# First stage of a hybrid decoder layer: x by token tile, conditioning in single chunks, loads in a fixed order

## The chip, the core and the metric

One core of a Trainium2 chip runs the whole layer in one launch. The metric is the device time of one execution in microseconds. TensorE (PE) multiplies into PSUM, VectorE (DVE), ScalarE (ACT) and GpSimd (POOL) work elementwise, SyncE (SP) issues most of the DMA loads.

## The reference

One layer of a decoder on x of 512 tokens by 1024, with a conditioning vector c of 1024. What the change touches is its beginning:

```
mod = silu(c) @ w_ada + b_ada            # w_ada: 1024 x 6144
shift_a, scale_a, gate_a, shift_f, scale_f, gate_f = split(mod, 6)
h = rms_norm(x, attn_norm) * (1 + scale_a) + shift_a
(nq, nkc, nvc, nks, nvs, nkw, nvw, ngate, cq, ckv, kr, bgate) = split(h @ w_in, ...)
```

After it come two attention branches (a sparse one with compressed, selected and window parts, and a latent one with a rotary key), gates, the output projection, and a gated MLP with a short causal convolution. Everything is float32; a product is made of three fp32r products of high and low halves (hi*hi, hi*lo, lo*hi).

## The kernel before

The kernel is written as a data flow of tiles. A planner orders the instructions of each engine ahead of the run, by priorities and its own estimate of times, and sets the semaphores; on the chip each engine runs its list in that order. `keep_in_program_order(ins)` binds an instruction behind the one that the program text traced before it on the same engine. `high_priority` moves it forward among those that are free to run.

The first stage computes the parts of `h @ w_in` that need all eight slices of 128 channels (k = 0 to 7) in seven PSUM banks at once: the gates and the latent query (408 columns, by token tile, banks bA) and the compressed keys and values (three of 128 columns, transposed, banks bF). Its pieces, in the text's order:

- x (eight DMAs of 256 KB, L417) is squared and summed per token, half on ACT (L437) and half on DVE (L434), the reciprocal root is taken on POOL for two token tiles at once (L135), and x is scaled. `x_half(i)` scales and transposes 512 channels of all four token tiles (L453, 16 transposes on PE) and copies them out of PSUM to xnT (L455). x_half(0) stands ahead of slice 0, x_half(1) behind its preparation.
- `mod_acc(j)` (L461) makes shift and scale for two slices at once: eight DMAs of 256 KB (L467: a row block of w_ada, two parts of 256 columns, 1 KB runs), and on DVE eight steps `acc = ada * csil[k] + acc` of 512 columns (L120, L122). The sum over the partitions follows in `mod_cols(j)` (L473): two f32 products with a column of ones on PE into a T bank, then mS and mA on DVE (L477 to L480).
- `prep(k)` calls both, loads and splits the weights of slice k (`load_w`: DMA at L112, high half by ACT at L83, low half by DVE at L84), issues late constants by the table LATE (L494), scales xnT[k] to h on ACT (L507) and splits h into hTh (ACT) and hTl (DVE).
- The loop at L517 calls prep(k + 1) and then issues slice k's 21 matmuls (L87): twelve of 408 columns and nine of 512.

The weight loads have 5 raw buffers, the conditioning loads 12 slots of 256 KB ("ml"), the split weights of this stage 10 ("cq"), the T banks of PSUM are two and one of them holds bF[2]. Only the late loads are bound to the text's order on SP. Behind the loop follow the latent query's norm, the second stage (banks bB, L555 on), the compressed branch, the eight heads and the MLP.

Of the kernel before, what the change touches and what calls it, by code (L numbers as in the profile page):

```python
# [10 lines left out]
F32 = mybir.dt.float32  # L11
# [6 lines left out]
P = 128  # L18
# [15 lines left out]
LATE = (0, 1, 1, 1, 2, 2, 2, 3, 3, 4, 5, 6, 7, 8, 9, 9, 9)  # L34
X_ACT = ((0, 0, 1, 1), (1, 1, 1, 1))
# [3 lines left out]
def tile_hybrid_layer(  # L39
# [18 lines left out]
    W_PRIO = [-50]  # L58
# [39 lines left out]

    @priority(lambda: W_PRIO[0])
    def load_w(segs, k0, kk, raw=None, tag=None):  # L100
        n = sum(g[2] for g in segs)
        assert kk * n <= 512
        raw = raw_unit() if raw is None else raw
        if tag:
            wh, wl = slot(tag, "wh", F32R), slot(tag, "wl", F32R)
        else:
            wh = wp.tile([P, 512], F32R, name="wh", tag="wh", bufs=4)
            wl = wp.tile([P, 512], F32R, name="wl", tag="wl", bufs=4)
        rv, hv, lv = (a[:, :kk * n].rearrange("p (k n) -> p k n", k=kk) for a in (raw, wh, wl))
# [299 lines left out]
    with tc.tile_pool(name="p1", bufs=1) as p1:  # L409
# [15 lines left out]
        vec.tensor_scalar(csil, csil, 0.5, None, op0=ALU.mult)  # L425

        ssh = sm.tile([P, NT, 2], F32, name="ssh")
        ssx = sm.tile([P, NT], F32, name="ssx")
        rsx = sm.tile([P, NT], F32, name="rsx")
        for t in range(NT):  # L430
            for i in range(2):
                if i:
                    scr = pj.tile([P, 512], F32, name="scr", tag="t2")
                    vec.tensor_tensor_reduce(scr, xt[t][i], xt[t][i], 1.0, 0.0, ALU.mult, ALU.add, ssh[:, t, i:i + 1])  # L434
                else:
                    scr = pj.tile([P, 512], F32, name="scr", tag="qg")
                    act.activation(scr, xt[t][i], AF.Square, accum_out=ssh[:, t, i:i + 1])  # L437
            if t % 2:
                t2 = slice(t - 1, t + 1)
                vec.tensor_add(ssx[:, t2], ssh[:, t2, 0], ssh[:, t2, 1])  # L440
                rstd(rsx[:, t2], ssx[:, t2], D, [P, 2])
        xnT = []

        def x_half(i):
            for t in range(NT):
                if X_ACT[i][t]:
                    act.activation(xt[t][i], xt[t][i], AF.Copy, scale=rsx[:, t:t + 1])
                else:
                    vec.tensor_scalar(xt[t][i], xt[t][i], rsx[:, t:t + 1], None, op0=ALU.mult)
            for k in range(4 * i, 4 * i + 4):  # L450
                tr = bank("T")
                for t in range(NT):
                    pe.transpose(tr[:, t * P:(t + 1) * P], xt[t][i][:, (k % 4) * P:(k % 4 + 1) * P], ident)  # L453
                xk = slot("KV", f"xnT{k}") if k < 6 else slot("KS", f"xnT{k}")[:, 0:512]
                act.activation(xk, tr, AF.Copy)  # L455
                xnT.append(xk)

        x_half(0)

        ACC = {}  # L460

        def mod_acc(j):
            if j % 2 == 0:
                acc = slot("U", "acc")
                for k in range(KD):
                    a = slot("ml", "ada")
                    dma(a.rearrange("p (s n) -> p s n", s=2),  # L467
                        w_ada[k * P:(k + 1) * P, 0:2 * D].rearrange("p (s n) -> p s n", s=2)[:, :, j * P:(j + 2) * P])
                    gemv_step(acc, a, k, True)
                for i in range(2):  # L470
                    ACC[j + i] = [acc[:, s * 256 + i * P:s * 256 + (i + 1) * P] for s in range(2)]

        def mod_cols(j):  # L473
            b = bank("T")
            for s in range(2):
                mm(b[:, s:s + 1], ACC[j][s], ones[:, 0:1], True, True)
            vec.tensor_add(mS[:, j:j + 1], b[:, 0:1], colA[:, 16 + j:17 + j])  # L477
            bp = sm.tile([P, 1], F32, name="bp")
            vec.scalar_tensor_tensor(bp, b[:, 1:2], 1.0, colA[:, 24 + j:25 + j], op0=ALU.add, op1=ALU.add)
            vec.tensor_mul(mA[:, j:j + 1], bp, colA[:, 8 + j:9 + j])  # L480
# [11 lines left out]
        def late_load(i):  # L492
            for dst, src in late[LATE[i]:LATE[i + 1]]:
                tc.keep_in_program_order(dma(dst, src))  # L494

        bA = [bank("G"), bank("G"), bank("S"), bank("S")]
        bF = [bank("O"), bank("F"), None]
        wk = {}

        def prep(k):  # L500
            mod_acc(k)
            mod_cols(k)
            wk[k] = (load_w([(w_in, O_NG, 408)], k, 1, slot("cq", "wr1")),
                     load_w([(w_in, O_KC, 384)], k, 1, slot("cq", "wr2")))
# [26 lines left out]
        pe.transpose(tr[:, 0:76], rowsB, ident[0:76, 0:76])  # L531
# [26 lines left out]
        for k in range(KD):  # L558
            wh, wl = load_w([(w_in, O_CKV, 320), (w_in, O_VC + P, P)], k, 1)
# [5 lines left out]
            mm3(bV1, wh[:, 0, 320:448], wl[:, 0, 320:448], hTh[k], hTl[k], st, sp)  # L565

# [555 lines left out]
```

## Time and profile before

| | us |
|---|---|
| three timed runs | 938.03, 938.11, 938.21 (median 938.11) |
| the profiled execution | 943.56 |
| its span, first to last instruction | 941.4 |

All numbers of a trace are from the profiled execution, counted from the start of its span. "Busy" is the time in which an engine had an instruction; matmuls overlap, so the time between two starts says more than the length of one. PEclk is the share of TensorE's full clock that was granted, 1.00 or 0.50 (2.4 or 1.2 GHz). In a row of the timeline, the brackets name what the engine waited for. x4 means four instructions merged into a row.

### The profile page before, as it was taken

To read this page: it belongs to the slowest core of one execution; us is meant where nothing else is said; L and a number is where in the kernel's file an instruction comes from. 1 tells how busy PE (TensorE), PEld (TensorE's weight loads), DVE (VectorE), ACT (ScalarE), POOL (GpSimd) and SP (SyncE) were. 2 spreads that over 40 slices of the span, in tenths; PEclk is the share of its full clock that TensorE was granted. 3 is DMA by queue.
4 is the path that set the end of the run, shared out by engine and by line. 5 is a ranking of instruction groups with operands and counts; after the bars stand their busy time and mean duration, and the time that the engine had idled before them with its cause. 6 is when DMAs were issued, how large, how long until landed. Compare 5 with 4: busy or idle time off the path is not lost.

```text
span 941.4 us, 15182 instructions
## 1 busy us (share of the span) xinstructions
PE 906.4 (96%) x5271; PEld 804.1 (85%) x5271; DVE 690.1 (73%) x1513; ACT 510.4 (54%) x1241; POOL 50.2 (5%) x57
## 2 busy tenths in 40 slices
PE   4899889999999999999999999999999999999998
PEld 3899888899999998989899899988888888888886
DVE  7868877888887789689967887797786667622423
ACT  5446757666775657568765654554444444422221
POOL 1000101010101001001001000000000000000000
PEclk9999999999999999999999999999999999999999
DMA  9934563532241262441214264263363333333421
GB/s 296 343 111 130 172 209 82 166 118 73 78 117 35 50 189 82 122 126 46 57 48 137 87 189 137 79 191 93 109 179 90 101 96 95 101 94 97 146 90 45
DMA packets 135778, 113.06 MB, mean 120 GB/s; under 512 B 7514, under 2 KB 118678, under 8 KB 135702
## 3 DMA queue, kind: packets, MB, share of 16 engines
q1 hardware_dynamic: 134934, 110.00, 39.3%
q0 software_dynamic: 768, 2.11, 0.7%
q8 instruction: 41, 0.67, 0.3%
q14 instruction: 35, 0.29, 0.1%
HBM read 109.98 MB, written 2.10 MB: 119 GB/s over the span
## 4 chain that ended last, share of the span: by engine, by line
PE 88%; DVE 4%; ACT 4%; DMA 3%; issue 1%; SPq 0%; DVEq 0%; ACTq 0%
PE psG L87 44%; PE psS L87 23%; PE psO L87 8%; PE psF L87 5%; PE psT L87 4%; PE psT L783 2%; DMA ada<-in_w_ada_dram 1%; DMA wr<-in_w_in_dram 1%; DVE wl L84 1%; ACT Pt L760 1%; ACT wh L83 1%; ACT sq L223 1%; DMA wr<-in_cmp_v_w_dram 0%; DVE acc L122 0%; SPq L417 0%
## 5 line engine op out<-in xcount | busy, mean ns | idle before, releaser
L83 ACT ACTIVATE wh<-wr 128x512 fp32r<-128x512 f32 (+3 forms) x304 | 186.9, 622 | 294.3 <-PE psS L87 101.8
L84 DVE TENSOR_TENSOR wl<-wr,wh 128x512 fp32r<-128x512 f32 (+3 forms) x304 | 203.2, 674 | 158.2 <-ACT wh L83 151.3
L87 PE MATMUL psG<-hTh,wh 128*128 128x512 f32 x192 | 76.6, 399 | 1.0 <-DVE qr L328 1.0
L87 PE MATMUL psG<-hTh,wl 128*128 128x512 f32 x192 | 76.3, 397 | 0.1
L87 PE MATMUL psG<-hTl,wh 128*128 128x512 f32 x192 | 76.3, 397 | 0.0
L87 PE MATMUL psS<-h2l,wh 128*128 128x512 f32 (+1 forms) x184 | 68.3, 371 | 0.0
L87 PE MATMUL psG<-h2h,wh 128*128 128x512 f32 (+1 forms) x184 | 68.2, 372 | 0.0
L87 PE MATMUL psS<-h2h,wl 128*128 128x512 f32 (+1 forms) x184 | 68.2, 371 | 0.0
L87 PE MATMUL psG<-h2h,wl 128*128 128x512 f32 (+1 forms) x184 | 68.2, 371 | 0.0
L87 PE MATMUL psG<-h2l,wh 128*128 128x512 f32 (+1 forms) x184 | 68.1, 371 | 0.0
L87 PE MATMUL psS<-h2h,wh 128*128 128x512 f32 (+1 forms) x184 | 68.0, 371 | 0.0
L760 ACT ACTIVATE Pt<-psS,nm 128x128 f32<-128x128 f32 (+2 forms) x96 | 51.3, 536 | 25.7 <-DVE nm L755 19.5
L122 DVE SCALAR_TENSOR_TENSOR acc<-wr,csil,acc 128x512 f32<-128x512 f32 x60 | 44.8, 746 | 3.1 <-DMA wr<-in_w_ada_dram 1.8
L84 DVE TENSOR_TENSOR PTl<-psT,PTh 128x384 fp32r<-128x384 f32 (+1 forms) x72 | 42.1, 596 | 6.7 <-ACT PTh L83 6.1
L83 ACT ACTIVATE PTh<-psT 128x384 fp32r<-128x384 f32 (+1 forms) x72 | 36.6, 530 | 17.8 <-PE psT L783 17.7
L87 PEld LDWEIGHTS psG<-hTh,wh 128*128 128x128 f32 x192 | 36.2, 188 | 7.6 <-PE psS L87 0.8
L87 PE MATMUL psG<-wh,hTh 128*128 128x256 f32 (+2 forms) x128 | 39.0, 315 | 3.8 <-ACT wh L83 2.4
L87 PEld LDWEIGHTS psG<-hTh,wl 128*128 128x128 f32 x192 | 36.1, 188 | 7.2 <-DVE wl L84 0.5
L87 PEld LDWEIGHTS psG<-hTl,wh 128*128 128x128 f32 x192 | 36.1, 188 | 6.4
L87 PE MATMUL psG<-wl,hTh 128*128 128x256 f32 (+2 forms) x128 | 39.9, 314 | 0.8 <-DVE wl L84 0.8
L87 PEld LDWEIGHTS psG<-h2h,wl 128*128 128x128 f32 x184 | 34.7, 189 | 6.1
L87 PEld LDWEIGHTS psG<-h2l,wh 128*128 128x128 f32 x184 | 34.6, 188 | 6.1
(431 smaller groups left out, 2593.6 us busy)
## 6 DMA issues: line engine op xcount, KB each, us to landing
wr<-in_w_up_dram SPq DMA_DIRECT2D x88, 256.0 KB, 2.9
wr<-in_w_ada_dram SPq DMA_DIRECT2D x64, 256.0 KB, 2.9
wr<-in_w_in_dram SPq DMA_DIRECT2D x48, 256.0 KB, 3.0
wr<-in_w_down_dram SPq DMA_DIRECT2D x44, 256.0 KB, 2.6
ada<-in_w_ada_dram SPq DMA_DIRECT2D x32, 256.0 KB, 5.4
wr<-in_w_o_dram SPq DMA_DIRECT2D x32, 256.0 KB, 2.8
wr<-in_w_in_dram SPq DMA_DIRECT2D x32, 128.0 KB, 3.0
wr<-in_cmp_k_w_dram SPq DMA_DIRECT2D x16, 256.0 KB, 3.2
```

The source lines that it names most:

```text
L83: act.activation(hi, src, AF.Copy)
L84: vec.tensor_sub(lo, src, f(hi))
L87: ins = pe.matmul(o, lhsT, rhs, start=start, stop=stop, skip_group_check=True)
L122: vec.scalar_tensor_tensor(acc, w, csil[:, k:k + 1], acc, op0=ALU.mult, op1=ALU.add)
L223: act.activation(sq[:, 0:n], b, AF.Square, accum_out=dst)
L760: act.activation(Pt[:, off[x2]:off[x2] + nt[x2]], Sb[x2], AF.Exp, bias=nm[:, x2:x2 + 1], scale=-1.0, accum_out=sums[:, x2:x2 + 1])
L783: pe.transpose(tr[:, e * P:(e + 1) * P], Pt[:, o:o + P], ident)
```

## The change

- x is normed and transposed by token tile: for each of the four tiles the two sums of squares, the root on POOL for this tile alone, both scalings, and the four transposes of its first 512 channels, into four banks (T, T, O, F). Slice 0 is scaled and split right out of its bank; slices 1 to 3 are copied out behind it; the other 512 channels follow in two calls of `x_half1`.
- `mod_acc` works on single slices for j = 0, 1, 2 and 7, with four DMAs of 256 KB each (four row blocks of 128 columns, 512-byte runs), and on pairs, as before, for (3, 4) and (5, 6). For j = 0 and 2 the sum is made on PE: sixteen f32 products of a 128x128 block with one column of csil. For j = 1 and 7 DVE does sixteen steps of 128 columns.
- The first DVE step of each conditioning chunk is bound behind what was traced before it on DVE, the first product of j = 2 behind the second token tile of slice 1, where prep(2) now stands.
- In this stage all loads on SP and the weight splits are in the text's order; `mod_cols` and the scaling and splitting of h have a high priority, as have the weight loads (W_PRIO 300 in place of -50). The first two weight pieces of the second stage are loaded with slice 7, the second stage's loads stay in order. Four small instructions behind it are bound in place.
- LATE moves vec_b and row_cq to slice 6 and tab to slice 7. 1 + b_ada for the scale is made once (bp1).

```diff
-LATE = (0, 1, 1, 1, 2, 2, 2, 3, 3, 4, 5, 6, 7, 8, 9, 9, 9)
+LATE = (0, 0, 0, 0, 0, 0, 0, 2, 3, 4, 5, 6, 7, 8, 9, 9, 9)
-    W_PRIO = [-50]
+    W_PRIO = [300]
+    W_PIN = [2]
+    pin = tc.keep_in_program_order
...
-    def split(hi, lo, src):
-        act.activation(hi, src, AF.Copy)
-        vec.tensor_sub(lo, src, f(hi))
+    def split(hi, lo, src, held=False):
+        a = act.activation(hi, src, AF.Copy)
+        b = vec.tensor_sub(lo, src, f(hi))
+        if held:
+            pin(a)
+            pin(b)
...
+            if W_PIN[0]:
+                pin(ld)
...
-    def gemv_step(acc, w, k, init):
+    def gemv_step(acc, w, k, init, pinned=False):
         if k == 0 and init:
-            vec.tensor_scalar(acc, w, csil[:, 0:1], None, op0=ALU.mult)
+            ins = vec.tensor_scalar(acc, w, csil[:, 0:1], None, op0=ALU.mult)
+            if pinned:
+                pin(ins)
...
+        trx = [bank(tag) for tag in ("T", "T", "O", "F")]
         for t in range(NT):
...
+            scr = pj.tile([P, 512], F32, name="scr", tag="qg")
+            act.activation(scr, xt[t][0], AF.Square, accum_out=ssh[:, t, 0:1])
+            scr = pj.tile([P, 512], F32, name="scr", tag="t2")
+            vec.tensor_tensor_reduce(scr, xt[t][1], xt[t][1], 1.0, 0.0, ALU.mult, ALU.add, ssh[:, t, 1:2])
+            vec.tensor_scalar(msx[:, t, 0:1], ssh[:, t, 0:1], 1.0 / D, EPS, op0=ALU.mult, op1=ALU.add)
+            vec.scalar_tensor_tensor(msx[:, t, 1:2], ssh[:, t, 1:2], 1.0 / D, msx[:, t, 0:1],
+                                     op0=ALU.mult, op1=ALU.add)
+            pool.tensor_tensor(rsx[:, t:t + 1], msx[:, t, 1:2], neghalf, op=ALU.pow)
+            vec.tensor_scalar(xt[t][0], xt[t][0], rsx[:, t:t + 1], None, op0=ALU.mult)
+            act.activation(xt[t][1], xt[t][1], AF.Copy, scale=rsx[:, t:t + 1])
+            for k in range(4):
+                pe.transpose(trx[k][:, t * P:(t + 1) * P], xt[t][0][:, k * P:(k + 1) * P], ident)
...
+        def ada_four(j, k, s):
+            a = slot("ml", "ada").rearrange("p (k n) -> p k n", k=4)
+            pin(dma(a, w_ada[k * P:(k + 4) * P, s * D + j * P:s * D + (j + 1) * P].rearrange("(k p) n -> p k n", p=P)))
+            return a
+
         def mod_acc(j):
-            if j % 2 == 0:
+            on_pe = j in (0, 2)
+            if j in (0, 1, 2, 7):
+                acc = bank("T" if j else "G") if on_pe else slot("U", "acc")
+                for k in range(0, KD, 4):
+                    for s in range(2):
+                        a = ada_four(j, k, s)
+                        for kk in range(k, k + 4):
+                            if on_pe:
+                                mm(acc[:, s:s + 1], a[:, kk - k, :], csil[:, kk:kk + 1], kk + s == 0, kk == KD - 1,
+                                   j and kk + s == 0)
+                            else:
+                                gemv_step(acc[:, s * P:(s + 1) * P], a[:, kk - k, :], kk, True, kk == 0)
+                ACC[j] = acc if on_pe else [acc[:, s * P:(s + 1) * P] for s in range(2)]
+            elif j in (3, 5):
...
-                    gemv_step(acc, a, k, True)
+                    gemv_step(acc, a, k, True, k == 0)
...
+        @priority(lambda: 300)
         def mod_cols(j):
...
         def prep(k):
             mod_acc(k)
-            mod_cols(k)
             wk[k] = (load_w([(w_in, O_NG, 408)], k, 1, slot("cq", "wr1")),
                      load_w([(w_in, O_KC, 384)], k, 1, slot("cq", "wr2")))
             late_load(k)
+            mod_cols(k)
+            h_split(k)
+
+        @priority(lambda: 300)
+        def h_split(k):
             h = pj.tile([P, 512], F32, name="h", tag="t1")
-            act.activation(h, xnT[k], AF.Identity, scale=mA[:, k:k + 1], bias=mS[:, k:k + 1])
             hh, hl = slot("hT", f"hTh{k}", F32R), slot("hT", f"hTl{k}", F32R)
-            split(hh, hl, h)
+            if k:
+                act.activation(h, xnT[k], AF.Identity, scale=mA[:, k:k + 1], bias=mS[:, k:k + 1])
+                split(hh, hl, h)
+            else:
+                act.activation(hh, trx[0], AF.Identity, scale=mA[:, 0:1], bias=mS[:, 0:1])
+                vec.tensor_scalar(h, trx[0], mA[:, 0:1], mS[:, 0:1], op0=ALU.mult, op1=ALU.add)
+                vec.tensor_sub(hl, h, f(hh))
...
         prep(0)
-        x_half(1)
+        for k in range(1, 4):
+            x_keep(k, trx[k])
+        x_half1(4, 6)
...
         for k in range(KD):
-            if k + 1 < KD:
+            if k + 1 < KD and k != 1:
                 prep(k + 1)
+            if k == KD - 2:
+                wB = [load_b(0), load_b(1)]
+                W_PIN[0] = 1
...
                 mm3(bA[t][:, 0:408], hh[:, ts], hl[:, ts], w1h[:, 0, :], w1l[:, 0, :], st, sp)
+                if k == 1 and t == 1:
+                    prep(2)
+                    x_half1(6, 8)
```

## Rows read from the trace of the kernel before

**Rows 1.** The page, part 1: busy us (share of the span) x instructions.

```profile
PE 906.4 (96%) x5271; PEld 804.1 (85%) x5271; DVE 690.1 (73%) x1513; ACT 510.4 (54%) x1241; POOL 50.2 (5%) x57
```

**Rows 2.** Busy time by stretch: its length, engines, granted clock, DMA share, GB/s.

```profile
17.00:23.00 6.00, 5.93 (x28) 5.04 (x27) 5.30 (x12) 4.64 (x9) 0.00 (x0) 1.00 1.10 344
...
30.30:33.60 3.30, 3.30 (x10) 3.13 (x10) 3.30 (x10) 1.45 (x2) 0.00 (x0) 0.50 1.08 371
...
45.00:47.00 2.00, 0.58 (x6) 0.47 (x4) 2.00 (x8) 1.86 (x3) 0.00 (x0) 1.00 0.85 316
47.00:65.00 18.00, 18.00 (x92) 16.55 (x93) 8.92 (x25) 9.91 (x25) 1.64 (x3) 1.00 0.42 125
...
84.00:130.00 46.00, 40.54 (x303) 38.28 (x302) 37.96 (x76) 31.25 (x81) 6.93 (x7) 0.95 0.60 177
130.00:941.00 811.00, 798.61 (x4625) 705.31 (x4624) 589.86 (x1286) 434.36 (x1074) 38.50 (x38) 1.00 0.36 106
```

**Rows 3.** The chain of waits, 0 to 140 us: start us, us, what.

```profile
5.29 6.02 DMA ada<-in_w_ada_dram
11.33 5.80 DMA wr<-in_w_in_dram
...
22.63 5.96 DMA ada<-in_w_ada_dram
...
45.43 0.81 ACT h L507
46.26 0.64 ACT hTh L83
...
64.55 0.47 PE psT L87 x2
```

**Rows 4.** PE's timeline, 0 to 80 us: start us, us, operation, idle before.

```profile
18.34 1.01 PE L87 MATMUL psT<-onesr,acc 128*128 128x1 f32 x4
19.24 4.11 PE L453 MATMUL psT<-ident,x 128*128 128x128 f32 x16
23.00 0.63 PE L87 MATMUL psG<-wh,hTh 128*128 128x408 f32 x1
...
29.63 0.61 PE L87 MATMUL psT<-onesr,acc 128*128 128x1 f32 x4 [1.10 <-DVE bp L479]
...
36.05 0.34 PE L87 MATMUL psG<-wh,hTh 128*128 128x408 f32 x1
...
40.30 0.34 PE L87 MATMUL psG<-wh,hTh 128*128 128x408 f32 x1
...
43.02 0.50 PE L87 MATMUL psT<-onesr,acc 128*128 128x1 f32 x4
43.38 0.43 PE L87 MATMUL psS<-wh,hTl 128*128 128x408 f32 x1
...
64.84 0.39 PE L87 MATMUL psT<-hTh,wl 128*128 128x512 f32 x1
```

**Rows 5.** DVE's timeline, 0 to 70 us.

```profile
3.85 0.17 DVE L424 SCALAR_TENSOR_TENSOR csil<-cth,colA 128x8 f32<-128x8 f32 x1 [0.28 <-ACT cth L423]
...
10.71 0.69 DVE L434 CUSTOM_DVE_ANT_0 scr<-x 128x512 f32<-128x512 f32 x1 [0.44 <-DMA x<-in_x_dram]
...
11.34 0.49 DVE L120 TENSOR_SCALAR acc<-ada,csil 128x512 f32<-128x512 f32 x1
...
41.35 2.32 DVE L122 SCALAR_TENSOR_TENSOR acc<-ada,csil,acc 128x512 f32<-128x512 f32 x3
43.59 0.15 DVE L477 TENSOR_TENSOR mS<-psT,colA 128x1 f32<-128x1 f32 x1
...
46.94 0.68 DVE L84 TENSOR_TENSOR hTl<-h,hTh 128x512 fp32r<-128x512 f32 x1
```

**Rows 6.** DMA issues by line: KB each, median us from issue to landing.

```profile
wr<-in_w_up_dram SPq DMA_DIRECT2D x88, 256.0 KB, 2.9
...
wr<-in_w_down_dram SPq DMA_DIRECT2D x44, 256.0 KB, 2.6
```

More of the change, by code (lines that the diff above doesn't have):

```diff
@@ L102, in load_w @@
         assert kk * n <= 512
+        held = W_PIN[0] > 1
         raw = raw_unit() if raw is None else raw
@@ L425, in tile_hybrid_layer @@
         vec.tensor_scalar(csil, csil, 0.5, None, op0=ALU.mult)
+        bp1 = p1.tile([P, KD], F32, name="bp1")
+        vec.tensor_scalar(bp1, colA[:, 24:32], 1.0, None, op0=ALU.add)
         ssh = sm.tile([P, NT, 2], F32, name="ssh")
-        ssx = sm.tile([P, NT], F32, name="ssx")
+        msx = sm.tile([P, NT, 2], F32, name="msx")
         rsx = sm.tile([P, NT], F32, name="rsx")
+        trx = [bank(tag) for tag in ("T", "T", "O", "F")]
         for t in range(NT):
[L431 to L450, printed above, removed]
+            scr = pj.tile([P, 512], F32, name="scr", tag="qg")
+            act.activation(scr, xt[t][0], AF.Square, accum_out=ssh[:, t, 0:1])
@@ L451, in x_half, with x_half1 @@
+        def x_half1(k0, k1):
+            for k in range(k0, k1):
                 tr = bank("T")
                 for t in range(NT):
[L453 to L458, printed above, removed]
+                    pe.transpose(tr[:, t * P:(t + 1) * P], xt[t][1][:, (k % 4) * P:(k % 4 + 1) * P], ident)
+                x_keep(k, tr)
@@ L466, in mod_acc @@
                     a = slot("ml", "ada")
-                    dma(a.rearrange("p (s n) -> p s n", s=2),
-                        w_ada[k * P:(k + 1) * P, 0:2 * D].rearrange("p (s n) -> p s n", s=2)[:, :, j * P:(j + 2) * P])
-                    gemv_step(acc, a, k, True)
+                    pin(dma(a.rearrange("p (s n) -> p s n", s=2),
+                            w_ada[k * P:(k + 1) * P, 0:2 * D].rearrange("p (s n) -> p s n", s=2)[:, :, j * P:(j + 2) * P]))
+                    gemv_step(acc, a, k, True, k == 0)
                 for i in range(2):
                     ACC[j + i] = [acc[:, s * 256 + i * P:s * 256 + (i + 1) * P] for s in range(2)]
+        @priority(lambda: 300)
         def mod_cols(j):
-            b = bank("T")
-            for s in range(2):
-                mm(b[:, s:s + 1], ACC[j][s], ones[:, 0:1], True, True)
+            if j not in (0, 2):
+                b = bank("T")
+                for s in range(2):
+                    mm(b[:, s:s + 1], ACC[j][s], ones[:, 0:1], True, True)
+            else:
+                b = ACC[j]
             vec.tensor_add(mS[:, j:j + 1], b[:, 0:1], colA[:, 16 + j:17 + j])
-            bp = sm.tile([P, 1], F32, name="bp")
-            vec.scalar_tensor_tensor(bp, b[:, 1:2], 1.0, colA[:, 24 + j:25 + j], op0=ALU.add, op1=ALU.add)
-            vec.tensor_mul(mA[:, j:j + 1], bp, colA[:, 8 + j:9 + j])
+            vec.scalar_tensor_tensor(mA[:, j:j + 1], b[:, 1:2], bp1[:, j:j + 1], colA[:, 8 + j:9 + j],
+                                     op0=ALU.add, op1=ALU.mult)
         rowsB = p1.tile([76, P], F32, name="rowsB")
@@ L558, in tile_hybrid_layer @@
         for k in range(KD):
-            wh, wl = load_w([(w_in, O_CKV, 320), (w_in, O_VC + P, P)], k, 1)
+            wh, wl = wB[k] if k < 2 else load_b(k)
             late_load(KD + k)
```

32 lines of the change are left out of this document (20 added, 12 removed).

## The prediction

> **What bounds the kernel now.** I read the page first: TensorE (PE) is busy 96% of the span [rows 1]. The table by stretches then shows where it is not: from 17 to 23 us PE looks busy, but with transposes and one-column products; from 45 to 47 us it is busy 0.58 of 2.00 us; from 47 to 65 us it never stops; from 130 us to the end it works 798.6 of 811 us [rows 2]. So what the first stage (line 517's loop, eight slices k of the first projections) costs is the time at which its last matmul ends, and a shift of that end passes nearly one to one to the end of the program. The chain of waits says what sets it: DMA of w_ada and w_in until 17.1 us, DMA of w_ada from 22.6 to 28.6, scaling and splitting on ScalarE (ACT) at 45.4 to 46.9, then only matmuls [rows 3]. The PE timeline gives the size: the first matmul of slice 0 starts at 23.00, a slice takes 40.30 - 36.05 = 4.25 us, and the last matmul starts at 64.84 and ends its slot 0.23 later, at 65.07 [rows 4]. Eight slices are 34.0 us, the stage takes 42.1 from its first matmul: 8 us are waits, half-rate clock, and small products between.
>
> **The changed stage, step by step.** I count from Tg, the moment at which the conditioning of slice 0 has come out of PE.
>
> *Tg itself.* Chunk 0 (1 MB, four DMAs) follows x in the queue. In the trace before the first w_ada piece is in at 11.3 us [rows 3], and at 344 GB/s [rows 2] a piece takes 0.76, so the fourth lands at 13.6. It now comes in 512-byte runs instead of 1 KB: w_up, also 512-byte runs, lands in a median 2.9 us against 2.6 for w_down with 2 KB runs [rows 6], so 0 to 0.3 us more a piece, 14.8 at most. PE then needs sixteen f32 products of one column; a conditioning read-out of two such products is four weight-load/matmul pairs [rows 4], so 32 pairs. Four pairs took 0.90 us at 18.34 and 0.36 at 43.02 [rows 4]: 0.225 or 0.09 each. The slow pace is PE at its lower level (1.2 GHz): the clock column prints 1.00 there, but the stretch at 30.3 with a granted clock of 0.50 shows the same stretching [rows 2], and the sixteen transposes behind 18.34 run at 4.11 / 16 = 0.257 each. Bounds: at the higher level 13.6 + 8 x 0.09 = 14.3; at the lower, eight transposes of x tiles 2 and 3 (2.05) and 32 x 0.225 = 7.2 from 11.3 give 20.6. From 16.5 to 23 us PE did this same mix and stayed at the slow pace, so I take 20.0, with some transposes done earlier.
>
> *x and slice 0.* Norm and transposes by token tile issue the same 32 transposes, eight scalings, eight square sums and some more small VectorE (DVE) steps of 0.15. The last x tile is summed from 10.71 [rows 5] and transposed by about 14.5, well before Tg: nothing on the path. Slice 0 is scaled straight out of PSUM, which saves one copy and one pass. Two small DVE steps (0.15 each) and one ACT pass of 0.81 [rows 3, 5] put its first matmul at Tg + 1.25 = 21.3, against 23.00: 1.7 us earlier. Its low half (one subtraction of 0.69) is done at Tg + 1.95.
>
> *Chunk 1 on DVE.* Its first step is held behind the instruction traced before it on DVE, and that is the subtraction of slice 0. It has 16 steps of 128 columns, which the trace does not show: a step of 8 columns takes 0.17 and one of 512 columns, each waiting for the one before, 2.32 / 3 = 0.77 [rows 5]. On the line between them 128 columns take 0.31; with 0.02 for the wait I take 0.33, and 5.2 us for all (bounds 16 x 0.2 = 3.2 and, at half of the wide pitch, 16 x 0.39 = 6.2). Done at Tg + 7.15. The handover is a read-out on PE (0.50), two small steps (0.3), scale (0.81), split (0.64) [rows 3 to 5] and five semaphores of 0.05 (the split ends at 46.90, the next engine starts at 46.94): 2.5. So slice 1 starts at Tg + 9.65, while slice 0 ended at Tg + 5.5: PE waits 4.1 us.
>
> The Trainium skill, "VectorE: DVE Perf Modes", section "The TRN2 errata", speaks against narrow steps too: each instruction pays a fixed latency, and tiles of 512 or more are advised. [...]
>
> *Chunk 2 on PE.* Its first product is pinned behind the first six matmuls of slice 1, whose low half is ready 0.7 after its start; these end at Tg + 10.8. 32 pairs at 0.09 are 2.9 us on PE (7.2 at the lower level), until Tg + 13.7. Scale and split (0.3 + 0.81 + 0.64 + 0.69 and semaphores) end at Tg + 16.25. PE meanwhile finishes slice 1 with eight transposes and slice 2 by about Tg + 22.05 (9.65 + 4.25 + 2.9 + 8 x 0.13 + 4.25).
>
> *Chunks 3 and 4.* Their steps on DVE are again held behind the last subtraction (slice 2), though their data are long there. One step of 0.49 and seven of 0.77 are 5.9: Tg + 22.15; the handover puts slice 3 at Tg + 24.65, a wait of 2.6 us. Slice 4 is scaled and split behind it, its low half ready at Tg + 26.85.
>
> *Chunks 5 and 6, chunk 7.* In the same way 5.9 us from Tg + 26.85, so slice 5 at Tg + 35.25 (PE ended slice 4 at 33.15: wait 2.1), and the low half of slice 6 at Tg + 37.4. Then sixteen narrow steps, 5.2, until Tg + 42.6; slice 7 at Tg + 45.1 (PE ended slice 6 at 43.75: wait 1.35) and its end at Tg + 49.35. In four handovers a weight split on DVE (a subtraction like the 0.68 of [rows 5], on fewer columns) may stand ahead of the two small steps: I add 1.0 together.
>
> *What costs nothing.* The conditioning loads of chunks 3 to 6 wait for the twelve slots of chunks 0 to 2, and w_in of slices 3 to 6 is queued behind them on SP; they land about Tg + 10 to Tg + 25, each before DVE turns to it. If this cover went, each MB would cost 3 us. The pinned late loads, the two early loads of the second stage and the transposes of vectors held back behind the stage are beside matmuls; a DVE that is busy 8.9 of 18 us from 47 to 65 [rows 2] has room. No work is taken off PE: it gains 64 pairs and loses two read-outs (8 pairs).
>
> **Sum.** End of the stage: 20.0 + 49.35 + 1.0 = 70.4 against 65.07, so 5.3 us later. On the profiled execution (943.56 us, span 941.4) that is 948.9; the three timed runs have a median of 938.11, 5.45 below it, and with the same difference I forecast 943.4. Its own range is 940.5 to 946.5.
>
> **Rivals.**
>
> *The waits are hidden (faster).* If DVE does the steps of the next chunk while ACT scales the last one, the waits of 4.1, 2.6, 2.1 and 1.35 us at slices 1, 3, 5, 7 go, and PE alone sets the end: Tg + 1.25 + 34.0 + 2.9 (chunk 2) + 2.2 (six read-outs of 0.36) + 2.0 (sixteen transposes of 0.13) = 62.35 at Tg = 20: 2.7 earlier, 935.4. It decides from the point at which more than 5.3 of the 10.2 us of waits are covered. For it: before, DVE already interleaves, and its 16 wide steps fewer leave it idle time. Against: the four holds, each behind a subtraction that itself needs the slice before.
>
> *The shift is swallowed (no change).* From 84 to 130 us PE is idle 46.00 - 40.54 = 5.5 us [rows 2]. If a later start lets the loads there run ahead, most of 5.3 goes: 938 to 940. Against: these loads are released by PE's own progress.
>
> *A colder PE (slower still).* After the gap at 29.63 PE had a granted clock of 0.50 for 3.3 us [rows 2, 4]. The 4 us gap ahead of slice 1 is longer; if chunk 2 then runs at 0.225 a pair, the path grows by 4.3: 947.7. By the Trainium skill ("TensorE: Matmul & The Clock Gate", "Why this matters for your kernels") idle gaps between bursts put PE back to half rate; the trace agrees with the 0.50.
>
> **Chances.** Forecast 0.42, colder PE 0.15, hidden waits 0.28, swallowed 0.15. A change within 0.2% (1.9 us) is about what a measurement cannot tell from none. Faster by more 0.28, within 0.13 (most of the swallowed case), slower 0.59. The range reaches from 934.2 to the colder PE, 947.7. Its low end holds the hidden waits and the cheapest case of the unknown costs: Tg = 14.3 alone gives an end at 64.65 and 937.7, and narrow steps at 3.2 instead of 5.2 take 2.0 at slice 1 and the 1.35 of slice 7 more. The dearest of them (Tg = 20.6, steps of 6.2 twice) gives 946.0.
>
> **What would show it.** Right: the first matmul of slice 0 at 20 to 22 us; PE waiting 2 to 4 us ahead of slices 1, 3, 5 and 7 for the scaled slice; narrow steps of 0.3 on DVE right behind a subtraction; the stage's last matmul near 70. Wrong: matmuls without a gap from 22 us and an end near 62; or a first matmul at 16 us, PE at its higher level while chunk 0 lands.

## The result, and the profile after

| | before | after |
|---|---|---|
| timed runs, median | 938.16 us | 963.64 us (961.42 to 966.47) |
| ratio of the two | | 1.0271, 95% interval 1.0239 to 1.0303 |
| profiled execution | 943.56 us | 965.08 us |
| first matmul of slice 0 | 23.00 us | 21.04 us |
| last matmul of the stage ends | 65.07 us | 86.09 us |

The changed kernel is slower by 25.5 us, where 5.3 were forecast. Some lines have moved in the changed kernel: the matmul of mm from L87 to L91, the high half of a split from L83 to L84 and the low half from L84 to L85, the conditioning steps from L120 and L122 to L127 and L131, the weight loads from L112 to L117.

The page's first part for the changed kernel, its row of engines and its row of granted clock in 40 slices, answers to [rows 1]:

```profile
PE 924.0 (96%) x5327; PEld 817.9 (85%) x5327; DVE 691.5 (72%) x1529; ACT 508.0 (53%) x1237; POOL 51.0 (5%) x59
...
PEclk9779999999999999999999999999999999999999
```

The same row of the clock in the kernel before:

```profile
PEclk9999999999999999999999999999999999999999
```

PE is busy 17.6 us more and DVE hardly. The two 7s are the clue: in before no slice of this row was below 9. The table by stretches of the changed kernel (columns as in [rows 2]), first the whole stage, then six places in it:

```profile
21.04:86.09 65.05, 55.48 (x236) 49.34 (x237) 37.47 (x91) 21.49 (x44) 0.55 (x1) 0.82 0.58 178
27.80:30.10 2.30, 0.01 (x1) 0.00 (x0) 0.72 (x4) 1.45 (x3) 0.00 (x0) 1.00 0.89 267
30.10:34.30 4.20, 4.16 (x13) 3.88 (x14) 1.65 (x3) 0.84 (x2) 0.00 (x0) 0.59 0.58 198
34.40:38.50 4.10, 4.10 (x34) 4.10 (x32) 0.00 (x0) 0.00 (x0) 0.00 (x0) 0.85 0.40 117
38.50:43.90 5.40, 5.40 (x17) 4.66 (x17) 3.61 (x7) 2.04 (x3) 0.00 (x0) 0.50 0.55 158
47.60:51.70 4.10, 1.82 (x14) 1.41 (x12) 1.57 (x7) 2.96 (x6) 0.00 (x0) 0.90 1.01 277
51.70:58.20 6.50, 6.50 (x19) 5.90 (x20) 5.74 (x10) 2.67 (x5) 0.00 (x0) 0.54 1.07 352
```

And the whole stage of the kernel before, in the same columns:

```profile
23.00:65.07 42.07, 39.55 (x198) 36.21 (x197) 29.96 (x72) 21.17 (x46) 1.64 (x3) 0.96 0.77 249
```

Such a row splits a stage in three. Length less PE's busy time is idle time: 9.6 us after, 2.5 before. One less the granted clock, times the length, is what the half clock (1.2 instead of 2.4 GHz) costs: 0.18 x 65.05 = 11.7 after, 1.7 before (the clock is printed to 0.01, so to 0.3 us). What is left is work at the full clock: 43.8 after, 37.9 before. So of the 21.0 us, 7.1 are waits, 10.0 are clock, 5.9 are added work (chunk 2's products, transposes that now lie between slices), and 2.0 come back from the earlier start. The rows below the first show how the two go together: a wait of 2.30 us, then matmuls at 0.59. They also show a fall without a wait: over the 32 one-column pairs (34.40 to 38.50) PE never stops and the mean is 0.85, so the clock fell at about 37.2, inside them.

The column misses one stretch. At the start of slice 0 it prints 1.00, but matmuls of 408 columns start 0.34 us apart there (21.54 and 21.88 below), as in the stretches at 0.50; at full clock it is 0.18 (80.42 to 80.60). The first eight matmuls of slice 0 take 2.75 us (21.04 to 23.79) against 1.76 in before (23.00 to 24.76), so up to 1.0 of the 5.9 us counted as work is half clock too.

PE's timeline of the changed kernel, the rows where it waits, and the products of chunk 2, answers to [rows 4]:

```profile
17.72 2.13 PE L91 MATMUL psG<-csil,ada 128*128 128x1 f32 x10
...
21.04 0.71 PE L91 MATMUL psG<-wh,hTh 128*128 128x408 f32 x1 [0.23 <-ACT hTh L545]
21.54 0.54 PE L91 MATMUL psG<-wl,hTh 128*128 128x408 f32 x1
21.88 0.54 PE L91 MATMUL psG<-wh,hTh 128*128 128x408 f32 x1
...
30.14 0.50 PE L91 MATMUL psG<-wh,hTh 128*128 128x408 f32 x1 [2.34 <-ACT hTh L84]
...
34.36 4.18 PE L91 MATMUL psT<-csil,ada 128*128 128x1 f32 x32
...
47.58 0.60 PE L467 MATMUL psT<-ident,x 128*128 128x128 f32 x4
48.87 0.61 PE L91 MATMUL psT<-onesr,acc 128*128 128x1 f32 x4 [0.69 <-ACT xnT L460]
50.11 0.61 PE L91 MATMUL psT<-onesr,acc 128*128 128x1 f32 x4 [0.64 <-DVE mA L510]
51.68 0.71 PE L91 MATMUL psG<-wh,hTh 128*128 128x408 f32 x1 [0.96 <-ACT hTh L84]
...
64.77 0.61 PE L91 MATMUL psT<-onesr,acc 128*128 128x1 f32 x4 [1.49 <-DVE acc L131]
...
67.49 0.45 PE L91 MATMUL psG<-wh,hTh 128*128 128x408 f32 x1 [0.96 <-ACT hTh L84]
...
77.69 0.50 PE L91 MATMUL psT<-onesr,acc 128*128 128x1 f32 x4
80.13 0.45 PE L91 MATMUL psG<-wh,hTh 128*128 128x408 f32 x1 [1.94 <-ACT hTh L84]
```

The waits lie ahead of slices 1, 3, 5 and 7, as forecast. DVE's timeline of the changed kernel, its conditioning steps, answers to [rows 5]:

```profile
21.86 0.69 DVE L547 TENSOR_TENSOR hTl<-h,hTh 128x512 fp32r<-128x512 f32 x1
22.47 0.28 DVE L127 TENSOR_SCALAR acc<-ada,csil 128x128 f32<-128x128 f32 x1
...
24.02 3.34 DVE L131 SCALAR_TENSOR_TENSOR acc<-ada,csil,acc 128x128 f32<-128x128 f32 x11
...
41.07 0.48 DVE L127 TENSOR_SCALAR acc<-ada,csil 128x512 f32<-128x512 f32 x1
41.59 5.47 DVE L131 SCALAR_TENSOR_TENSOR acc<-ada,csil,acc 128x512 f32<-128x512 f32 x7
...
54.50 0.48 DVE L127 TENSOR_SCALAR acc<-ada,csil 128x512 f32<-128x512 f32 x1
55.02 4.69 DVE L131 SCALAR_TENSOR_TENSOR acc<-ada,csil,acc 128x512 f32<-128x512 f32 x6
63.83 0.23 DVE L672 CAST maskr<-qs 128x128 bf16<-128x128 f32 x1 [4.12 <-DMA qs<-in_tab_dram]
63.97 0.75 DVE L131 SCALAR_TENSOR_TENSOR acc<-ada,csil,acc 128x512 f32<-128x512 f32 x1
...
70.32 0.28 DVE L127 TENSOR_SCALAR acc<-ada,csil 128x128 f32<-128x128 f32 x1
...
71.87 3.35 DVE L131 SCALAR_TENSOR_TENSOR acc<-ada,csil,acc 128x128 f32<-128x128 f32 x11
```

Each chunk starts right behind a subtraction (hTl). And the seventh of seven steps of chunks 5 and 6 stands behind a copy of the mask that has nothing to do with it. The chain of waits of the changed kernel over that place answers to [rows 3] (start us, us, what):

```profile
53.03 6.58 DMA wr<-in_w_in_dram
...
60.99 2.81 DMA qs<-in_tab_dram
...
63.83 0.04 DVE maskr L672
...
63.97 0.06 DVE acc L131
```

The load of the mask went out in its place on SP at 60.99, behind the first weight loads of the second stage (from 53.03 on), so the copy stood on DVE for 4.12 us, and the conditioning behind it. Nothing of the change touches what [rows 6] show.

### The profile page after: what moved, and what is told of

Its sections match the earlier page's. It is cut to its first block, busy times and chain, and to the rows that moved or that the text cites. A ratio compares the mean times of both kernels' runs of the same rounds, so it can differ in the third digit from the quotient of the medians.

```text
span 963.0 us, 15287 instructions
## 1 busy us (share of the span) xinstructions
PE 924.0 (96%) x5327; PEld 817.9 (85%) x5327; DVE 691.5 (72%) x1529; ACT 508.0 (53%) x1237; POOL 51.0 (5%) x59
## 4 chain that ended last, share of the span: by engine, by line
PE 82%; ACT 6%; DVE 5%; DMA 4%; issue 2%; SPq 1%; DVEq 0%; ACTq 0%
PE psG L91 40%; PE psS L91 22%; PE psO L91 7%; PE psF L91 4%; PE psT L91 4%; PE psT L836 2%; DMA wr<-in_w_in_dram 2%; DVE wl L85 2%; ACT Pt L813 1%; ACT wh L84 1%; SPq L117 1%; ACT sq L232 1%; DVE acc L131 1%; SPq L474 1%; DMA x<-in_x_dram 1%
## 5 line engine op out<-in xcount | busy, mean ns | idle before, releaser
L84 ACT ACTIVATE wh<-wr 128x512 fp32r<-128x512 f32 (+3 forms) x304 | 186.2, 621 | 291.0 <-PE psS L91 97.2
L85 DVE TENSOR_TENSOR wl<-wr,wh 128x512 fp32r<-128x512 f32 (+3 forms) x304 | 202.4, 673 | 158.1 <-ACT wh L84 151.0
L91 PE MATMUL psG<-hTh,wh 128*128 128x512 f32 x192 | 76.6, 399 | 1.0 <-DVE qr L337 1.0
L91 PE MATMUL psG<-hTh,wl 128*128 128x512 f32 x192 | 76.3, 397 | 0.1
L91 PE MATMUL psG<-hTl,wh 128*128 128x512 f32 x192 | 76.2, 397 | 0.0
L91 PE MATMUL psS<-h2l,wh 128*128 128x512 f32 (+1 forms) x184 | 68.4, 371 | 0.0
L91 PE MATMUL psG<-h2h,wh 128*128 128x512 f32 (+1 forms) x184 | 68.2, 372 | 0.0
L91 PE MATMUL psS<-h2h,wl 128*128 128x512 f32 (+1 forms) x184 | 68.2, 371 | 0.0
L91 PE MATMUL psG<-h2h,wl 128*128 128x512 f32 (+1 forms) x184 | 68.2, 371 | 0.0
L91 PE MATMUL psG<-h2l,wh 128*128 128x512 f32 (+1 forms) x184 | 68.1, 371 | 0.0
L91 PE MATMUL psS<-h2h,wh 128*128 128x512 f32 (+1 forms) x184 | 68.0, 371 | 0.0
L91 PE MATMUL psG<-wh,hTh 128*128 128x256 f32 (+2 forms) x128 | 39.7, 318 | 10.7 <-ACT hTh L84 6.2
L85 DVE TENSOR_TENSOR PTl<-psT,PTh 128x384 fp32r<-128x384 f32 (+1 forms) x72 | 42.1, 596 | 6.7 <-ACT PTh L84 6.2
L131 DVE SCALAR_TENSOR_TENSOR acc<-wr,csil,acc 128x512 f32<-128x512 f32 x60 | 44.6, 744 | 3.0 <-DMA acc<-in_b_ada_dram 2.3
L84 ACT ACTIVATE PTh<-psT 128x384 fp32r<-128x384 f32 (+1 forms) x72 | 36.6, 529 | 16.5 <-PE psT L836 16.4
L91 PEld LDWEIGHTS psG<-hTh,wh 128*128 128x128 f32 x192 | 36.2, 188 | 7.5 <-PE psS L91 0.7
L91 PEld LDWEIGHTS psG<-hTh,wl 128*128 128x128 f32 x192 | 36.1, 188 | 7.2 <-DVE wl L85 0.6
L91 PEld LDWEIGHTS psG<-hTl,wh 128*128 128x128 f32 x192 | 36.2, 188 | 6.4
L91 PE MATMUL psG<-wl,hTh 128*128 128x256 f32 (+2 forms) x128 | 39.7, 312 | 0.2 <-DVE wl L85 0.2
L91 PEld LDWEIGHTS psS<-h2h,wh 128*128 128x128 f32 x184 | 34.7, 189 | 6.0
L91 PEld LDWEIGHTS psG<-h2h,wl 128*128 128x128 f32 x184 | 34.7, 189 | 6.0
```

The lines of the kernel that those rows point to most:

```text
L84: a = act.activation(hi, src, AF.Copy)
L85: b = vec.tensor_sub(lo, src, f(hi))
L91: ins = pe.matmul(o, lhsT, rhs, start=start, stop=stop, skip_group_check=True)
```

## The experiments

All beside the kernel before on the same chip (median 938.2 to 939.1 us in four sets). The kernels named e_ and h_ are edits of the changed kernel, those named b_ of the kernel before.

**e_mask.** The copy of the mask is bound behind a memset which itself is free to run at 1 us, so the binding holds it nowhere. Here the memset is bound too.

```diff
-        vec.memset(maskr[:, 0:384], 0.0)
+        pin(vec.memset(maskr[:, 0:384], 0.0))
```

> The changed kernel with one small thing more: the memset of the mask's left part is bound in place too, so that the mask's copy, bound behind it, no longer stands in VectorE's list between the conditioning steps of chunks 5/6, where it waited 4.1 us for its DMA. Theory H (the holds of the conditioning steps make most of the loss, the mask's wait is a part by itself): the last step of chunk 5/6 follows at once, slice 5 starts 4 us earlier, the stage ends near 81, time 958 to 960 (of 963.6). Theory D (the first stage is held up by late loads anyway, the mask's wait only shows it): another DMA wait takes its place there and the time stays within 1 us of 963.6.

Measured 960.83 us (1.0237, 1.022 to 1.0254): 2.8 less by the medians, but the timed runs overlap (960.10 to 962.30 against 961.42 to 966.47). In its trace the seven steps are one row again, and the whole stage ends at 81.76, 4.3 us earlier:

```profile
53.62 0.48 DVE L127 TENSOR_SCALAR acc<-ada,csil 128x512 f32<-128x512 f32 x1
54.14 5.48 DVE L131 SCALAR_TENSOR_TENSOR acc<-ada,csil,acc 128x512 f32<-128x512 f32 x7
```

```profile
21.36:81.76 60.40, 52.88 (x237) 47.63 (x237) 37.65 (x90) 21.50 (x44) 0.55 (x1) 0.86 0.62 190
```

Slice 5 starts at 64.67, 2.8 us earlier and not 4: its read-out now stands on PE behind slice 4. The wait is a part of the loss by itself, as theory H has it; its price, 2.8, is the roughest figure here.

**e_free.** No conditioning step is held.

```diff
-gemv_step(acc[:, s * P:(s + 1) * P], a[:, kk - k, :], kk, True, kk == 0)
+gemv_step(acc[:, s * P:(s + 1) * P], a[:, kk - k, :], kk, True)
...
-gemv_step(acc, a, k, True, k == 0)
+gemv_step(acc, a, k, True)
```

> The changed kernel without the holds of the conditioning steps on VectorE (the first step of each chunk is free again); all else stays, the mask's copy too. Theory H: VectorE does chunks 3/4 while TensorE does chunk 2, the waits of TensorE ahead of slices 1, 3, 5 and 7 (2.3, 4, 4.6 and 2 us) shrink to under 1 us each and the half-clock stretches behind them go with them: the stage ends at 62 to 68, time 938 to 946. Theory D (loads late, because the order on SyncE is fixed and buffers come free late): the waits turn into waits for DMA, the stage ends above 78, time above 956. Theory P (chunk 2 on TensorE at half clock is the main part): about 955.

Measured 949.97 us (1.012, 1.0097 to 1.0144): 13.7 less, the largest single step, but 11.8 us over before remain. No theory's range holds it: the holds cost most, as in H, yet 4 us more are left than H allows, and the stage ends at 74.17 and not by 68.

**e_free_mask.** Both edits.

> Both edits: no holds on the conditioning steps, and the mask's copy out of the stage. Theory H: as without holds, and up to 4 us less where the mask's copy still waited: 934 to 942, the stage ends at 60 to 65. If the mask's copy now stands where its data are there, no difference to the kernel without holds (within 1.5 us).

Measured 952.09 us (1.0146, 1.0124 to 1.0168). Theory H's 934 to 942 is missed by 10 us; the 2.1 us to e_free are within what the two intervals allow. With the holds gone the mask's copy still waits (2.88 us at 55.10 in e_free), but no conditioning step is behind it; binding it gains nothing more.

**e_dve2.** Chunk 2 is worked out on DVE, holds and all else as in the change.

```diff
-            on_pe = j in (0, 2)
+            on_pe = j == 0
...
-            if j not in (0, 2):
+            if j:
```

> The changed kernel with chunk 2 on VectorE (sixteen steps of 128 columns, held like the others) in place of TensorE; slice 2 is still prepared behind the second token tile of slice 1. Theory H: its 4.8 us on VectorE start right behind the low half of slice 1 (at 30.8) and end at 35.6 in place of 38.5, so 3 us less, and TensorE, which then waits ahead of slice 2 in place of working, loses some of it again: 960 to 963. Theory P (32 one-column pairs on TensorE among the matmuls and their half clock are the main loss): 955 or less.

Measured 959.63 us (1.0219, 1.0199 to 1.0239): 4.0 less, at the cheap edge of theory H and clear of theory P's 955.

**e_all.** The three edits above, and the preparation of slice 2 and the last transposes of x ahead of slice 1's matmuls.

```diff
-            if k + 1 < KD and k != 1:
+            if k + 1 < KD:
                 prep(k + 1)
+            if k == 1:
+                x_half1(6, 8)
...
-                if k == 1 and t == 1:
-                    prep(2)
-                    x_half1(6, 8)
```

> The changed kernel with four things undone: no conditioning step is held in program order, the memset of the mask is held beside its copy, chunk 2 is worked out on DVE, and the preparation of slice 2 and the last two transposes of x stand ahead of slice 1's matmuls as for every other slice. Theory A (what is left of the loss once the holds are gone is chunk 2 at PE's low clock and the read-out of chunk 3 that waits for a T bank behind the late transposes): the stage ends at 66 to 70 us, so 939 to 944 us, with no PE gap over 1.5 us between slices 1 and 5. Rival R (the rest is the single chunks themselves: their loads, their narrow steps and the clock after slice 0): the gaps stay, the stage ends at 73 to 76 us, 948 to 952 us.

Measured 943.89 us (1.0053, 1.0038 to 1.0068), at the dearer end of theory A, though the stage ends at 64.88, earlier than the 66 to 70 of that theory. 19.8 of the 25 us are gone.

**h_all.** e_all with the holds put back.

> As the kernel with four things undone (943.9 us), but with the conditioning steps held in program order again; mask held, chunk 2 on DVE and the preparation of slice 2 in its normal place stay. Theory H (the holds keep each chunk's steps behind the splits and read-outs of the chunk before, whatever the order around them, and this is the largest single part): PE waits 2 us or more for the split of hTh ahead of most slices, the stage ends at 72 to 80 us, 951 to 959 us. Rival (the holds hurt only together with chunk 2 on PE or with the late place of slice 2's preparation): 943 to 947 us.

Measured 956.82 us (1.0198, 1.0184 to 1.0212): the holds cost 12.9 us by themselves. The whole stage of h_all and then of e_all, columns as above:

```profile
21.18:78.09 56.91, 46.31 (x209) 41.19 (x209) 42.04 (x106) 20.98 (x44) 0.55 (x1) 0.91 0.66 201
```

```profile
22.26:64.88 42.62, 41.15 (x208) 37.24 (x209) 34.10 (x87) 20.97 (x44) 0.55 (x1) 1.00 0.84 263
```

Idle 10.6 against 1.5, clock 5.1 against nothing, the rest 41.2 in both; 1.1 earlier at the start. That is 9.1 + 5.1 - 1.1 = 13.1 us, near the price measured. So the holds cost nine us of waits and another five at the half clock behind them.

**e_free_normal2** and **e_dve2_mask_free** take the other two edits apart. The first is e_all with chunk 2 on PE, the second e_all with slice 2's preparation in the changed place.

> The changed kernel without holds on the conditioning steps, with the memset of the mask held, and with the preparation of slice 2 and the last transposes of x ahead of slice 1's matmuls; chunk 2 stays on PE. Theory A: the T bank for the read-out of chunk 3 is free early, the 2.4 us gap before slice 3 goes, but slice 1 now stands behind chunk 2's 32 products (4.2 us at 0.13 us each): 943 to 948 us. Rival R (place of the preparation is nothing, chunk 2 on PE is the whole rest): 949 to 953 us, as without the move.

> As the kernel with four things undone (943.9 us), but the preparation of slice 2 and the last two transposes of x stand again after half of slice 1, as in the changed kernel. Theory A2 (the place alone costs nothing once chunk 2 is on DVE, and what looked like its price was chunk 2 on PE): 942 to 946 us. Rival P (the place has a price of its own, since the read-out of chunk 3 stands behind those transposes and waits for their T bank): 947 to 951 us, with a PE gap over 2 us ahead of slice 3.

Measured 951.80 us (1.0137, 1.0122 to 1.0152) and 944.26 us (1.0059, 1.0046 to 1.0071). The place is worth nothing, 952.09 against 951.80 with chunk 2 on PE and 944.26 against 943.89 with it on DVE. In the first run theory A was wrong and its rival right; in the second theory A2 holds. Chunk 2 on PE alone is 7.8 us once the holds are gone. Its sixteen f32 products, 32 load/matmul pairs, take 3.6. PE's timeline of e_free_normal2, and then the clock around it:

```profile
29.47 3.62 PE L91 MATMUL psT<-csil,ada 128*128 128x1 f32 x32
...
44.91 0.60 PE L91 MATMUL psT<-onesr,acc 128*128 128x1 f32 x4 [0.69 <-ACT xnT L460]
47.22 0.60 PE L91 MATMUL psT<-onesr,acc 128*128 128x1 f32 x4 [1.71 <-DVE mA L510]
48.67 1.01 PE L91 MATMUL psT<-onesr,acc 128*128 128x1 f32 x4 [0.84 <-DVE mA L510]
```

```profile
32.00:34.00 2.00, 2.00 (x16) 2.00 (x16) 2.00 (x6) 0.00 (x0) 0.00 (x0) 1.00 1.06 342
34.00:36.00 2.00, 2.00 (x8) 1.95 (x7) 1.50 (x3) 1.45 (x2) 0.00 (x0) 0.58 1.10 349
36.00:38.00 2.00, 2.00 (x7) 1.57 (x7) 1.97 (x4) 0.00 (x0) 0.00 (x0) 0.57 1.09 351
...
50.00:52.00 2.00, 2.00 (x7) 1.94 (x7) 1.84 (x5) 1.22 (x2) 0.00 (x0) 0.50 0.94 283
```

The clock falls at 34.3, 1.3 us behind the last of the 32 one-column pairs, though PE has had no idle time since slice 0 began at 21.35; it falls again at 48 us, behind the waits of 0.69 and 1.71. And the last rows show a second cost. The read-out of chunk 3 stands on PE behind transposes of x; when it has run, the two small steps that take it up stand on DVE behind the narrow steps of chunk 7, the first of which waited for its load until 43.62:

```profile
43.62 0.29 DVE L127 TENSOR_SCALAR acc<-ada,csil 128x128 f32<-128x128 f32 x1 [2.11 <-DMA ada<-in_w_ada_dram]
```

The whole stage of e_free_mask and then of e_dve2_mask_free, which differ by chunk 2 alone:

```profile
22.08:75.71 53.63, 50.31 (x236) 45.58 (x237) 33.45 (x78) 22.87 (x48) 1.65 (x3) 0.87 0.67 211
```

```profile
22.16:65.22 43.06, 41.93 (x209) 38.09 (x209) 34.26 (x87) 20.85 (x44) 0.55 (x1) 1.00 0.81 258
```

Idle +2.2, clock +7.0, work +1.4: within the stage the work that PE took over is the smallest part of what it cost. The stage is 10.6 us longer, the kernel 7.8 (6.9 between the two profiled executions): behind the stage e_free_mask takes 875.6 us and e_dve2_mask_free 879.2, and no run shows why.

The two prices hang on each other. With the mask bound, both the holds and chunk 2 on PE give 960.83 (e_mask), chunk 2 on PE alone 952.09 (e_free_mask), the holds alone 956.82 (h_all), neither 944.26. So the holds are worth 8.7 us with chunk 2 on PE and some 12.6 without, and chunk 2 on PE 4.0 us with the holds and 7.8 without. The half clock of these four stages goes the same way, by the column 8.5, 7.0, 5.1 and nothing: either is enough to bring it, and the two do not add up.

**e_all_pairs and e_all_s2** look for the last 5 us: the first makes the conditioning of every two chunks together on DVE, as before, the second undoes what the change did to the hand-over to the second stage.

```diff
-            on_pe = j == 0
+            on_pe = False
-            if j in (0, 1, 2, 7):
+            if False:
-            elif j in (3, 5):
+            elif j % 2 == 0:
```

```diff
-LATE = (0, 0, 0, 0, 0, 0, 0, 2, 3, 4, 5, 6, 7, 8, 9, 9, 9)
+LATE = (0, 1, 1, 1, 2, 2, 2, 3, 3, 4, 5, 6, 7, 8, 9, 9, 9)
-                wB = [load_b(0), load_b(1)]
-                W_PIN[0] = 1
+                W_PIN[0] = 0
-            wh, wl = wB[k] if k < 2 else load_b(k)
+            wh, wl = load_b(k)
```

(and the four bound instructions behind the stage free again).

> As the kernel with four things undone (943.9 us), but every two chunks of the conditioning are worked out together on DVE, in wide steps, as in the kernel before; loads in the text's order. Rival L (single chunks cost through their narrow steps of 0.30 us for 128 columns against 0.67 to 0.78 us for 512): 940 to 942 us. Theory S: 943 to 945 us, since the first stage ends within 1 us of the kernel before already.

> As the kernel with four things undone (943.9 us), and with the hand-over to the second stage as in the kernel before: the late loads at their old places, the first loads of the second stage not brought forward, no load held from slice 6 on, the transposes and scalings behind the stage not held. Theory S (of the 5 us that are left, some 3 are lost behind the first stage, because that work now lies beside the second stage): 940 to 942 us. Rival L (the 5 us come from the first stage's own order of loads and its single chunks): 943 to 945 us.

Measured 941.67 us (1.0032, 1.0021 to 1.0044) and 946.96 us (1.0087, 1.0074 to 1.01). The pairs give 2.2 us back, as rival L has it. Theory S fell: undoing the hand-over made the kernel 3.1 slower, which rival L (943 to 945) did not forecast either, and its stage ends at 69.9 us. DVE there waits 3.23 us for a conditioning load at 52.05: chunk 7's loads went out on SP from 43.79, right behind the late load of tab (833 KB) at 43.27, and took a median 8.6 us to land.

**b_x, b_prio, b_xp, b_order** each put one part of the change into the kernel before: x by token tile; the priority of read-out, scaling and split; both; the order of the loads.

```diff
+        @priority(lambda: 300)
         def mod_cols(j):
...
+        @priority(lambda: 300)
+        def h_split(k):
```

```diff
+            if W_PIN[0]:
+                tc.keep_in_program_order(ld)
```

> The kernel before with one part of the change alone: x normed and transposed by token tile as it lands, the first four transposed chunks kept from four banks; conditioning in pairs, nothing else moved. Theory A (this part is no cause of the loss; slice 0 is bound by its conditioning, which is not touched): 937 to 940 us, slice 0 starts within 1 us of 18.3. Rival X (four banks are held until the read-outs and the transposes of the second half stand between slices): 942 to 948 us with a PE gap ahead of slice 1 or 2.

> The kernel before with one part of the change alone: read-out of the conditioning, scaling and split of each slice go ahead of ordinary work in the planner's order. Theory A (before loses 1.9 us ahead of slice 4 because its read-out stands late on PE; earlier read-outs give that back, and nothing else of the stage moves): 935 to 938 us. Rival (an earlier place in PE's list makes PE wait for DVE in order, as in the changed kernel): 939 to 945 us.

> The kernel before with the two parts of the change that cost nothing alone: x normed and transposed by token tile, and the read-outs, scaling and splits of the conditioning put ahead in the planner's order. Conditioning stays in pairs and nothing is held. Theory A (each moved the end of the stage by 0 to 2 us earlier and the next stage gave most of it back): 935.5 to 939 us. Rival (together they hold four banks while the read-outs want one): 940 to 944 us.

> The kernel before with one part of the change alone: the loads of the first stage go out in the order of the text only. Theory S (order of loads costs nothing; DMA is ahead of its users in the first stage): 938 to 940 us. Rival L: 941 to 944 us.

Measured 939.03 (1.0006, 0.9997 to 1.0016), 938.60 (0.9999, 0.9989 to 1.0009), 938.84 (1.0001, 0.9992 to 1.001) and 944.62 us (1.0066, 1.0054 to 1.0079). Two parts of the change are worth nothing, alone and together, though b_prio and b_xp end the stage at 62.9 and 63.1: their second stage's first matmul then waits 0.95 for ACT. For b_prio theory A had forecast 935 to 938. (The 18.3 in the expectation of b_x is where the first read-out starts; slice 0 starts at 23.00 in before and 23.36 in b_x.) The order of the loads alone costs 5.9, against theory S and 0.6 above the range of rival L. In e_all_pairs, whose loads are bound to the text's order too, 2.9 are lost in all.

**b_same.** The kernel before, unchanged, profiled again.

> The kernel before, unchanged, profiled a second time. Its first profiled execution took 943.56 us where its median is 938.1 to 939.0. If that execution was disturbed by its two stretches at half clock (30.3 to 33.6 us, and a mean of 0.95 between 84 and 130 us), this one takes 937 to 940 us, shows neither, and its first stage ends at 62 to 64 us rather than 65.1. If the profile itself costs the 5 us, it takes 942 to 945 us again.

It took 939.79 us. Its whole stage, columns as above:

```profile
23.89:64.19 40.30, 38.57 (x198) 35.33 (x197) 29.72 (x72) 20.96 (x46) 1.64 (x3) 1.00 0.78 251
```

The column shows no half clock in the stage (only the first five matmuls of slice 0 still stand at the slow pace, until 25.67, which it misses as in the changed kernel), the end is 0.9 earlier, and 875.6 us follow it, where the first profile had 878.5. From 84 to 130 us the clock is 0.96 again, so that stretch was no disturbance. The execution on which the forecast rests was 3.8 us longer than this one, most of it behind the stage. Against b_same the changed kernel's profile is 21.9 us later at the stage's end and 3.4 behind it (965.08 - 86.09 = 879.0), together the 25.3 that the timed runs show.

No kernel run here beats the one before by more than can be measured.

## Why the prediction was wrong

Its direction and one mechanism held: conditioning steps held behind subtractions make PE wait ahead of slices 1, 3, 5 and 7. The size failed, because of a term that the sum does not have: each slice was put at 4.25 us, the full clock, and the half clock took 11.7. Step by step:

- *Tg* 20.0: 19.85. The one-column products ran at the slow pace, 0.21 a pair. *Slice 0* 21.3: 21.04. *Chunk 1* 5.2 us, slice 1 at 29.65: 4.8 us (0.30 a step), slice 1 at 30.14. All right. The Trainium skill ("VectorE: DVE Perf Modes", "The TRN2 errata") has (N + 151) cycles at 0.96 GHz for an fp32 tensor_tensor add; by it 128 columns would take an estimated 0.29 us and 512 an estimated 0.69. The rows of these scalar_tensor_tensor steps, each waiting for the one before, show 0.30 and 0.78 (5.47 / 7).
- *Chunk 2 on PE*, 2.9 us, done at 33.7: 4.18 us, done at 38.5, since it started 3.6 us later than forecast, behind thirteen matmuls of slice 1, most at half clock, where I had counted six. From here all that follows is late, because the next chunk is held behind slice 2's subtraction.
- *Chunks 3 and 4*, 5.9 us: 41.07 to 47.0, 5.9. *The handover*, 2.5: 4.6, slice 3 at 51.68 instead of 44.65. The read-out stands on PE behind four transposes of x and waits until ACT has copied their bank out (47.58 to 48.87 above), and a weight split stands on DVE ahead of the small steps. I had allowed 1.0 for all four handovers.
- *Chunks 5 and 6*, 5.9: 10.1, slice 5 at 67.49 instead of 55.25. This is the step "What costs nothing". It said that the pinned late loads are beside matmuls and that "a DVE that is busy 8.9 of 18 us ... has room". DVE did have room; but its list is in order, and an instruction that waits for a load holds all behind it. e_mask prices it: 2.8, by the medians.
- *Chunk 7*, 5.2: 4.8. Its handover was 5.0 long, as the read-out stood behind all of slice 6 (77.69). Slice 7 at 80.13 instead of 65.1, and it took 5.96 instead of 4.25.

The waits were forecast too small by 2.6 us together: 4.1 + 2.6 + 2.1 + 1.35 + 1.0 = 11.2 from the end of one slice to the start of the next, against 2.9 + 4.1 + 4.4 + 2.4 = 13.8 (27.27 to 30.14, 47.58 to 51.68, 63.12 to 67.49, 77.69 to 80.13), of which PE was idle 9.5 and otherwise at read-outs and transposes. That the sums lie so near is in part luck: the wait ahead of slice 1 is shorter only since slice 0 ended at 27.27 instead of 25.5.

The step that failed most is the one that the working never named as such: each slice at 4.25 us, the full clock, although four gaps of 1 to 4 us were forecast in front of them and the profile had shown half clock behind a gap of 1.1. Of the 15.7 us by which the stage ended later than forecast (86.09 against 70.4), the half clock is 11.7. It was a rival ("a colder PE", 947.7), but there for chunk 2 alone, 4.3 us. The runs with the mask bound show that it comes with the holds' gaps (5.1 in h_all, nothing in e_all) and with chunk 2 on PE (7.0 in e_free_mask, nothing in e_dve2_mask_free), and that either alone brings more than half of what both bring (8.5 in e_mask). The Trainium skill ("TensorE: Matmul & The Clock Gate", "Why this matters for your kernels") puts the loss on idle gaps between bursts. The trace agrees in kind behind the gap of 2.30 (0.59), though that gap is shorter than those the page warns of; at 34.3 us of e_free_normal2 the clock fell where no gap was, and of such a fall that section says nothing.

The other rivals: the hidden waits need the holds gone, and even then chunk 2 on PE kept 5.7 to 7.8 us (e_free and e_free_mask against e_dve2_mask_free). Nothing was swallowed behind the stage; 3.4 us were added there. And one sum of the range is off by a little, with no weight: 937.7 less 2.0 and 1.35 is 934.35, not 934.2.

What stays open: the last 5 us. The profiled executions say where they lie: e_all is 3.3 us longer than b_same, 0.7 of it until the stage ends (64.88 against 64.19) and 2.6 behind it; the pairs give 2.2 back, and e_all_pairs has 876.3 us behind the stage, e_all 878.2. b_order, with a stage end of 65.36, has 878.9 there, so the order of the loads alone can cost as much behind the stage (one profile of each). Which edit makes the 2.6 was not split, nor why the time behind the stage lies anywhere from 875.0 (e_free) to 879.2 (e_dve2_mask_free). By which edit the read-out of a chunk could be put ahead of the transposes with chunk 2 still on PE was not tried.

## What to carry to other kernels

Price a gap on PE twice, once as the wait and once as the work behind it at half clock: the gaps of the holds cost 9.1 us as waits and 5.1 more as half clock (h_all against e_all). An instruction bound in an engine's order must have its data early, or everything behind it on that engine waits for its load. Before giving PE small products because it is idle, look at what they do to its clock: here 3.6 us of products cost 7.8 (4.0 where the holds stayed), and taking them back and freeing the held steps returned 20 of the 25 us.

## What was not expected of the hardware

- The granted clock fell to 0.50 with no idle time ahead of the fall, 1.3 us behind the last of 32 one-column load/matmul pairs (34.3 us in e_free_normal2); in the changed kernel it fell inside the pairs (about 37.2 us) and stayed at 0.50 from 38.5 to 43.9.
- The clock column prints 1.00 at the start of slice 0 in the changed kernel and in b_same, while the matmuls there start 0.34 us apart, the pace of the stretches at 0.50.
- Gaps of the same size are not alike: behind 1.10 us at 29.63 in the first profile of before the clock fell for 3.3 us [rows 2, 4], behind 1.42 at 46.94 it did not, and behind 1.50 at 45.56 in b_order it fell to a mean of 0.57 from 46 to 50 us.
